# One level of Strassen in the gate and up projections of a decoder layer, with the down projection by tokens and its sum in DRAM

## The chip, the cores and the metric

The kernel runs on one core of one Trainium2 chip. The metric is the device time of one execution in microseconds (us). TensorE (PE) multiplies; a matmul holds a 128x128 stationary operand (loaded by a weight load, PEld) and streams a moving operand of up to 512 columns past it into one of eight PSUM banks. VectorE (DVE), ScalarE (ACT) and GpSimd (POOL) work on SBUF and PSUM; DMAs are issued from the queues of SyncE (SP), ACT and POOL.

## The reference

One layer of a decoder with 512 tokens, model width 2048, feed-forward width 5632, in fp32:

```python
x = x + concat(diff_attention(...), retention(...)) @ w_o       # from one combined projection w_in of rmsnorm(x)
x = x + cross_attention(rmsnorm(x), rmsnorm(mem)) @ w_xo        # 256 memory tokens, 4 heads
hf = rmsnorm(x, norm_ffn_g)
x = x + (silu(hf @ w_gate) * (hf @ w_up)) @ w_down
return rmsnorm(x, norm_f_g)
```

The change is in the feed-forward part, the third and fourth lines; its three weight matrices hold 3 x 2048 x 5632 numbers.

## The kernel before

**Precision.** Each fp32 operand is written as a sum of two `float32r` halves, `hi` (a rounded copy, made by ACT) and `lo` (the rest, made by DVE); `split` does it. A product is three matmuls, hi·hi, hi·lo and lo·hi (`mm3`, lines 129 to 131).

**Weights as a stream.** All weights are cut on the host into chunks of 128 x 1024 (512 KB), in the order in which they are used. `plan` is a list of chunks written out by the code at the end; `run_plan` goes through it. At chunk i it issues loads up to chunk i+5 (`raw`, four buffers, SP queue), splits up to chunk i+2 (`hi`, `lo`, three buffers each), then the matmuls of chunk i (`use`), then the evacuation of its banks if the chunk is the last of its group (`evac`), then one step of every side generator. Each engine runs its instructions in the order in which they are recorded here; semaphores do the rest.

**Stages.** Memory projections (matmuls with 256 moving columns), then eight heads with their projections ("mix"), cross attention, its output projection (`plan_xo`, 16 chunks), and the feed-forward part in eleven blocks b of 512 features. `plan_gate(b)` and `plan_up(b)` are 8 chunks each, `plan_down(b)` is 8 chunks in 4 groups. The order is gate(0), up(0), then gate(b), down(b-1), up(b) for b = 1 to 10.

**Feed-forward before.** Activations are feature-major: `xT[k]` holds 128 features by 512 tokens. In `feature_major` the stationary operand is a weight block and the moving operand is `ah[k]`/`al[k]` (the halves of `xT[k]` times the gain, 512 columns). A gate or up block takes 16 x 4 x 3 = 192 matmuls of 512 columns into four banks. The four gate banks are multiplied by `r_bc` (the norm's 1/rms, spread over partitions; DVE line 726), put through Silu (ACT 728) and multiplied by `r_bc` again (DVE 729); the up banks are multiplied by that (DVE 738) and split into `live["a"]`. `plan_down` is feature-major as well and adds each bank to the residual `xT[k]` (DVE 746). The last down block (b = 10) is left to `finish`: its weights are split by `last_weights` into `ah`/`al`, the residual is turned to token-major by 64 transposes (`turn_residual`), and 192 matmuls, token by token, give the rows that are normed and stored.

Of the kernel before, what the change touches and what calls it, by code (L numbers as in the profile page):

```python
# [35 lines left out]
LOADS_AHEAD = 6  # L36
# [4 lines left out]
LINE = 32  # L41
# [22 lines left out]
def hybrid_block_kernel(ctx, tc, specs, x_t, mem_t, gains, norm_f_g, weights, alibi, decay, out):  # L64
# [6 lines left out]
    res = ctx.enter_context(tc.tile_pool(name="res", bufs=1))  # L71
    wp = ctx.enter_context(tc.tile_pool(name="wp", bufs=1))
    dram = ctx.enter_context(tc.tile_pool(name="dram", bufs=1, space=DRAM))
    ps_acc = ctx.enter_context(tc.tile_pool(name="ps_acc", bufs=4, space=PSUM))
    ps_aux = ctx.enter_context(tc.tile_pool(name="ps_aux", bufs=4, space=PSUM))

    def acc(name="acc"):
        return ps_acc.tile([P, 512], F32, tag="acc", name=name)

    def aux(name="aux"):  # L80
        return ps_aux.tile([P, 512], F32, tag="aux", name=name)

    phase = ExitStack()
    mp = phase.enter_context(tc.tile_pool(name="mp", bufs=1))
# [6 lines left out]
    gc = const.tile([P, 96], F32, name="gc")  # L91
    nc.scalar.dma_start(out=gc[:, :NG], in_=gains)
    lam2 = const.tile([P, LINE], F32, name="lam2")[:, :2]
    elam = const.tile([P, LINE], F32, name="elam")[:, :2]
    lam = const.tile([P, LINE], F32, name="lam")[:, :1]
    gsub = const.tile([P, LINE], F32, name="gsub")[:, :2]

# [16 lines left out]
    def tmp():  # L114
        return wp.tile([P, T], F32, tag="tmp", name="tmp", bufs=2)
# [17 lines left out]
    def rsqrt(dst, ss, n, pool):  # L133

        w = dst.shape[-1]
        v = pool.tile([P, LINE], F32, tag="rs_v", name="rs_v")[:, :w]
        nh = pool.tile([P, LINE], F32, tag="rs_h", name="rs_h")[:, :w]
        y = pool.tile([P, LINE], I32, tag="rs_y", name="rs_y")[:, :w]
        t = pool.tile([P, LINE], F32, tag="rs_t", name="rs_t")[:, :w]
# [14 lines left out]
    def across(dst, cols):  # L154
# [7 lines left out]
        b_ps = aux("b_ps")  # L162
# [5 lines left out]
    def token_sums(dst, sq):  # L168

        s_ps = aux("s_ps")  # L170
# [6 lines left out]
    plan = []  # L177
    raws, halves, side = {}, {}, []
    count = {"load": 0, "split": 0}

# [3 lines left out]
    def load(i):  # L184
        raw = wp.tile([P, 1024], F32, tag="raw", name="raw", bufs=4)
        raws[i] = raw
        for a, b in pieces_of(i):
            nc.sync.dma_start(out=raw[:, a:b], in_=plan[i]["src"][:, a:b])

    def halve(i):  # L190
        raw = raws.pop(i)
        hi = wp.tile([P, 1024], F32R, tag="hi", name="hi", bufs=3)
        lo = wp.tile([P, 1024], F32R, tag="lo", name="lo", bufs=3)
        for a, b in pieces_of(i):
            split(hi[:, a:b], lo[:, a:b], raw[:, a:b])
        halves[i] = (hi, lo)
# [10 lines left out]
    def load_more(upto):  # L207
        while count["load"] < min(upto, len(plan)):
# [3 lines left out]
    def split_more(upto):  # L212
        while count["split"] < min(upto, len(plan)):
            halve(count["split"])
            count["split"] += 1

    def run_plan():
        for i, c in enumerate(plan):
            for f in c["early"]:
                f()  # L220
            load_more(i + LOADS_AHEAD)
            split_more(i + SPLITS_AHEAD)
            for f in c["before"]:
                f()
            c["use"](*halves.pop(i))
# [9 lines left out]
    def add(src, use, evac, hook):  # L235
        plan.append({"src": src, "use": use, "evac": evac, "hook": hook, "early": [], "before": [], "side": "after"})
# [34 lines left out]
    def token_major(w, width, nk_total, lhs_of, ntok, finish, hook=None, bank=acc):  # L271
# [3 lines left out]
        for k0 in range(0, nk_total, nk):  # L275
            last = k0 + nk >= nk_total

            def use(hi, lo, k0=k0, last=last):
# [8 lines left out]
                (lambda: [finish(t, banks[t]) for t in range(ntok)]) if last else None, hook if last else None)  # L287


    xT = [res.tile([P, T], F32, name=f"xT{k}") for k in range(KT)]  # L290
    ah = [res.tile([P, T], F32R, name=f"ah{k}") for k in range(KT)]
    al = [res.tile([P, T], F32R, name=f"al{k}") for k in range(KT)]
    ssq = const.tile([P, T], F32, name="ssq")
    rx = const.tile([P, LINE], F32, name="rx")[:, :NT]
    rxs = const.tile([P, LINE], F32, name="rxs")[:, :NT]
    g_d = dram.tile([HEADS // 2, KT // 2, P, 1024], F32, name="g_d")
    h_d = dram.tile([D // 512, HEADS, P, 1024], F32, name="h_d")

# [7 lines left out]
    mh = [mp.tile([P, MEM], F32R, name=f"mh{k}") for k in range(KT)]  # L306
    ml = [mp.tile([P, MEM], F32R, name=f"ml{k}") for k in range(KT)]
    rm = mp.tile([P, LINE], F32, name="rm")[:, :MT]
    rm_bc = mp.tile([P, MEM], F32, name="rm_bc")
# [8 lines left out]
    def start():  # L318
        for j in range(4):
            load_mem(j)  # L320
            load_more(j + 1)
# [9 lines left out]
    def mem_stats():  # L331
# [9 lines left out]
        sm2 = mp.tile([P, LINE], F32, name="sm2")[:, :MT]  # L341
        nc.vector.tensor_copy(sm2, s_ps[:, :MT])
        rsqrt(rm, sm2, D, mp)
# [6 lines left out]
    def plan_memory(h):  # L350
# [3 lines left out]
        def fin_x(name):  # L354
            def fin(o, ps):
                if o == 0:
                    xs[name] = (mp.tile([P, 4, MEM], F32R, tag=name + "h", name=name + "h", bufs=1),
                                mp.tile([P, 4, MEM], F32R, tag=name + "l", name=name + "l", bufs=1))
# [5 lines left out]
        for c in range(4):  # L364
            def fin_h(t, ps, c=c):
                if t == 0:
                    xs["h"] = mp.tile([P, 2, 512], F32, tag="mst", name="hst", bufs=3)
# [7 lines left out]
        for c in range(4):  # L375
            def fin_g(o, ps, c=c):
                if o == 0:
                    xs["g"] = mp.tile([P, 4, MEM], F32, tag="mst", name="gst", bufs=3)
# [15 lines left out]
    def prepare_x():  # L394
# [9 lines left out]
        st4 = wp.tile([P, LINE], F32, tag="st4", name="st4", bufs=1)[:, :NT]  # L404
        token_sums(st4, ssq)
        yield
        rsqrt(rx, st4, D, wp)
# [13 lines left out]
    pool = {}  # L421

    def half_pair(tag, shape, bufs=1):
        return (pool[0].tile(shape, F32R, tag=tag + "h", name=tag + "h", bufs=bufs),
                pool[0].tile(shape, F32R, tag=tag + "l", name=tag + "l", bufs=bufs))

# [3 lines left out]
    def plan_values(h):  # L430
# [5 lines left out]
        def fin_vg(t, ps):  # L436
            fin_v(t, ps)
            if t == 0:
                live["g", h] = pool[0].tile([P, NT, 256], F32, tag="gate", name="gate", bufs=1)
# [19 lines left out]

    def head_norm(om, ss):  # L460
        rs = pool[0].tile([P, LINE], F32, tag="rs", name="rs", bufs=1)[:, :NT]
        rsqrt(rs, ss, 256, pool[0])
        return rs
# [14 lines left out]
    def diff_head(h):  # L478
        qk = live["qk", h]
        tab = pool[0].tile([P, 640], F32, tag="tab", name="tab", bufs=1)  # L480
        nc.sync.dma_start(out=tab[:, :T], in_=alibi[h])
        om = pool[0].tile([P, NT, 256], F32, tag="om", name="om", bufs=1)
        ss = pool[0].tile([P, LINE], F32, tag="ss", name="ss", bufs=1)[:, :NT]
# [12 lines left out]
        def exps(i):  # L496
            n = (i + 1) * P
            e = pool[0].tile([P, 2, (P, 2 * P, T, T)[i]], F32, tag=("e3", "e1", "gate", "e3")[i], name="e", bufs=1)
            st = pool[0].tile([P, LINE], F32, tag="st", name="st", bufs=4)
# [45 lines left out]
        steps = ((0, scores), (3, turn), (5, values), (1, exps), (2, combine), (4, halve_weights), (6, collect))  # L545
# [12 lines left out]
    def ret_head(h):  # L558
        qk = live["qk", h]
        tab = pool[0].tile([P, 640], F32, tag="tab", name="tab", bufs=1)  # L560
        nc.sync.dma_start(out=tab, in_=decay[h - 4])
        om = pool[0].tile([P, NT, 256], F32, tag="om", name="om", bufs=1)
        ss = pool[0].tile([P, LINE], F32, tag="ss", name="ss", bufs=1)[:, :NT]
# [12 lines left out]
        for p in range(2):  # L576
            nj = 2 * p + 2
            i0 = p * 256
            st = pool[0].tile([P, nj, 256], F32, tag=("e1", "e3")[p], name="rst", bufs=1)
# [47 lines left out]
    prep = {"done": KT, "ready": 0, "gen": None}  # L627

    def prepare(at):
# [11 lines left out]
        st4 = wp.tile([P, LINE], F32, tag="st4", name="st4", bufs=1)[:, :NT]  # L641
        token_sums(st4, ssq)
        yield
        rsqrt(rx, st4, D, wp)
        nc.vector.tensor_scalar(out=rxs, in0=rx, scalar1=float(SX), scalar2=None, op0=ALU.mult)

    def start_prepare(at):
        prep["gen"] = prepare(at)
# [3 lines left out]
    def prepared_rhs(k):  # L652
        while prep["done"] <= k:
            next(prep["gen"])
        return ah[k], al[k]

# [3 lines left out]
    def plan_scores(p):  # L660
# [5 lines left out]
        def fin(t, ps):  # L666
            if t == 0:
                sc = pool[0].tile([P, 4, NT, 2], F32, tag="xst", name="xst", bufs=2)
                live["p", p] = (pool[0].tile([P, NT, 2, MEM], F32, tag="xe", name="xe", bufs=2), sc)
# [47 lines left out]
    turns = [0]  # L717

    def alternate():
        turns[0] += 1  # L720
        return (acc, aux)[turns[0] % 2 == 0]

    def plan_gate(b):
        def fin(o, ps):
            t = tmp()
            nc.vector.tensor_tensor(out=t, in0=ps, in1=live["r_bc"], op=ALU.mult)
            s = pool[0].tile([P, T], F32, tag=f"gs{o}", name="gs", bufs=1)
            nc.scalar.activation(s, t, AF.Silu)
            nc.vector.tensor_tensor(out=s, in0=s, in1=live["r_bc"], op=ALU.mult)
            live["s", o] = s  # L730
        feature_major(cols("w_gate", (b * 512, 512)), 512, KT, prepared_rhs, T, fin, bank=alternate())

    def plan_up(b):
        def fin(o, ps):
            if o == 0:
                live["a"] = half_pair("a", [P, 4, T])
            s = live["s", o]
# [185 lines left out]
```

## Time and profile before

| | |
|---|---|
| median of 3 runs | 2801.92 us (2801.42 to 2802.19) |
| the profiled execution | 2801.72 us, of which the span of the trace is 2799.9 us |
| TensorE | 2782.8 us busy (99%), 13910 matmuls |
| VectorE / ScalarE | 1290.0 us (46%) / 859.2 us (31%) |
| feed-forward part | from about 1337 us to the end |
| one block of it (gate, down, up) | 131.85 us |

How to read it: a matmul's own duration in the trace (391 ns for 512 columns) overlaps with the next one's, so what counts on TensorE is the distance from one start to the next. "Idle before" of an engine names what it waited for. Rows of a timeline begin with the start in us and the duration.

### The profile page before, as it was taken

What the parts mean: (1) busy time and instruction counts of PE and PEld (TensorE: products, weight loads), DVE (VectorE), ACT (ScalarE), POOL (GpSimd) and SP (SyncE); (2) the same over time, 40 slices, a digit from 0 to 9 for tenths busy, and PEclk for the clock granted to TensorE, in tenths of its full rate; (3) what the DMA queues carried; (4) which work ended last, traced back from release to release, by engine and by line L of the source; (5) the groups of instructions that cost most, each with busy time, mean ns of one, the idle gap of its engine ahead of it and who ended that gap; (6) DMA issues with size and microseconds to landing.
All of it is one profiled execution on the core that took longest, in us unless ns stands there. A gap on an engine that the chain in (4) does not pass through costs nothing.

```text
span 2799.9 us, 33522 instructions
## 1 busy us (share of the span) xinstructions
PE 2782.8 (99%) x13910; PEld 2358.7 (84%) x13910; DVE 1290.0 (46%) x1855; ACT 859.2 (31%) x1182; POOL 3.0 (0%) x10
## 2 busy tenths in 40 slices
PE   9999999999999999999999999999999999999998
PEld 8999988888888888888888888888888888888886
DVE  6676444544543444745433434343434243434356
ACT  5555433332322222434221212222222222222223
POOL 0000000000000000000000000000000000000000
PEclk9999999999999999999999999999999999999999
DMA  7877652222222222222223222222222222222241
GB/s 242 288 241 227 216 188 84 87 87 94 88 91 89 94 91 90 96 90 95 94 91 102 94 98 98 91 98 98 98 94 94 98 98 95 94 98 98 92 134 68
DMA packets 99192, 322.29 MB, mean 115 GB/s; under 512 B 10592, under 2 KB 20832, under 8 KB 99040
## 3 DMA queue, kind: packets, MB, share of 16 engines
q1 hardware_dynamic: 96272, 310.68, 33.4%
q10 hardware_dynamic: 2448, 8.43, 0.7%
q8 instruction: 109, 1.79, 0.3%
q0 software_dynamic: 320, 1.05, 0.1%
q14 instruction: 43, 0.35, 0.0%
HBM read 299.14 MB, written 20.97 MB: 114 GB/s over the span
## 4 chain that ended last, share of the span: by engine, by line
PE 98%; DVE 1%; ACT 0%; issue 0%; DMA 0%; ACTq 0%; DVEq 0%
PE fm L129 26%; PE fm L131 26%; PE fm L130 26%; PE tm L129 5%; PE tm L130 5%; PE tm L131 5%; PE y L130 1%; PE y L129 1%; PE y L131 1%; PE mx_ps L472 0%; PE y_ps L778 0%; DVE xT L620 0%; PE at_ps L523 0%; PE s_ps L130 0%; PE s_ps L129 0%; PE s_ps L131 0%
## 5 line engine op out<-in xcount | busy, mean ns | idle before, releaser
L121 DVE TENSOR_TENSOR lo<-raw,hi 128x1024 fp32r<-128x1024 f32 (+1 forms) x545 | 666.1, 1223 | 1211.9 <-ACT hi L120 1198.1
L120 ACT CAST hi<-raw 128x1024 fp32r<-128x1024 f32 (+1 forms) x545 | 572.1, 1050 | 1589.9 <-PE fm L130 1293.5
L129 PE MATMUL fm<-ah,hi 128*128 128x512 f32 x2432 | 951.6, 391 | 0.0
L131 PE MATMUL fm<-ah,lo 128*128 128x512 f32 x2432 | 950.3, 391 | 0.0
L130 PE MATMUL fm<-al,hi 128*128 128x512 f32 x2432 | 950.2, 391 | 0.0
L131 PEld LDWEIGHTS fm<-ah,lo 128*128 128x128 f32 x2432 | 456.5, 188 | 99.4
L129 PEld LDWEIGHTS fm<-ah,hi 128*128 128x128 f32 x2432 | 456.6, 188 | 98.2
L130 PEld LDWEIGHTS fm<-al,hi 128*128 128x128 f32 x2432 | 456.6, 188 | 98.1
L129 PE MATMUL tm<-hi,ah 128*128 128x512 f32 (+1 forms) x640 | 222.6, 348 | 0.6 <-DVE qkl L121 0.3
L130 PE MATMUL tm<-lo,ah 128*128 128x512 f32 (+1 forms) x640 | 221.9, 347 | 0.0
L131 PE MATMUL tm<-hi,al 128*128 128x512 f32 (+1 forms) x640 | 221.9, 347 | 0.0
L129 PE MATMUL fm<-mh,hi 128*128 128x256 f32 x512 | 146.5, 286 | 6.2 <-ACT hi L120 6.2
L131 PE MATMUL fm<-mh,lo 128*128 128x256 f32 x512 | 145.6, 284 | 0.0
L130 PE MATMUL fm<-ml,hi 128*128 128x256 f32 x512 | 145.5, 284 | 0.0
L746 DVE TENSOR_TENSOR xT<-xT,fm 128x512 f32<-128x512 f32 x160 | 109.8, 686 | 61.5 <-PE fm L131 56.9
L129 PEld LDWEIGHTS tm<-hi,ah 128*128 128x128 f32 x640 | 121.2, 189 | 16.0 <-issue 0.7
L131 PEld LDWEIGHTS tm<-hi,al 128*128 128x128 f32 x640 | 121.2, 189 | 15.1
L130 PEld LDWEIGHTS tm<-lo,ah 128*128 128x128 f32 x640 | 121.2, 189 | 14.6
L129 PEld LDWEIGHTS fm<-mh,hi 128*128 128x128 f32 x512 | 97.9, 191 | 6.4 <-ACT hi L120 6.2
L620 DVE TENSOR_TENSOR xT<-xT,fm 128x512 f32<-128x512 f32 x128 | 85.2, 683 | 32.4 <-PE fm L131 30.7
L131 PEld LDWEIGHTS fm<-mh,lo 128*128 128x128 f32 x512 | 97.7, 191 | 0.2 <-DVE lo L121 0.2
L130 PEld LDWEIGHTS fm<-ml,hi 128*128 128x128 f32 x512 | 97.8, 191 | 0.0
(202 smaller groups left out, 2426.4 us busy)
## 6 DMA issues: line engine op xcount, KB each, us to landing
raw<-in_weights_dram SPq DMA_DIRECT2D x519, 512.0 KB, 3.3
h_d<-hst ACTq DMA_DIRECT2D x16, 512.0 KB, 5.4
g_d<-gst SPq DMA_DIRECT2D x32, 256.0 KB, 3.6
raw<-g_d SPq DMA_DIRECT2D x16, 512.0 KB, 3.2
raw<-h_d SPq DMA_DIRECT2D x16, 512.0 KB, 3.2
xT<-in_x_t_dram SPq DMA_DIRECT2D x16, 256.0 KB, 5.0
out_dram<-xT SPq DMA_DIRECT2D x16, 256.0 KB, 2.6
xT<-in_mem_t_dram SPq DMA_DIRECT2D x8, 256.0 KB, 6.9
```

The costliest lines, as they stand in the source:

```text
L120: nc.scalar.copy(hi, src)
L121: nc.vector.tensor_tensor(out=lo, in0=src, in1=hi.bitcast(F32), op=ALU.subtract)
L129: nc.tensor.matmul(out_ap, lh, rh, start=first, stop=False)
L130: nc.tensor.matmul(out_ap, lh, rl, start=False, stop=False)
L131: nc.tensor.matmul(out_ap, ll, rh, start=False, stop=last)
L620: nc.vector.tensor_tensor(out=xT[k], in0=xT[k], in1=ps, op=ALU.add)
L746: nc.vector.tensor_tensor(out=xT[k], in0=xT[k], in1=ps, op=ALU.add)
```

## The change

**Gate and up.** Let the activations be cut into halves of the contraction (two k tiles of a pair j) and halves of the tokens, and the weights into halves of the contraction and of the 512 output columns. The four block products of each gate or up block become seven products of half size (`PRODUCTS`). Each uses one of seven sums of weight quarters and one of seven sums of activation quarters. `combine_weights` makes the weight sums of each chunk (DVE 266, 268, 269) and splits all seven (ACT 267, 270; DVE 271, 272), 1792 columns in place of 1024. `prepare_pairs` makes the activation sums once for all blocks. `seven_products` then issues 42 matmuls of 256 columns per chunk (7 products x 2 output tiles x 3 halves; the seven results lie in seven PSUM banks), where there were 24 of 512 columns. At the end of a block the four quarters of the result are put together from the seven banks (line 899 and 902 on DVE, one copy on ACT), for gate in `fin` with the norm and Silu in the side generator `activate`, for up in `fin` and `rest_of`.

**Down.** `token_major`: the stationary operand is the activation `a`, the moving one the weights (512 columns, as many matmuls as before). ACT takes each bank to SBUF times `rx` (line 974), into one of the two buffers of `tmp`, and a DMA on the POOL queue adds it to `y_d` in DRAM (line 975, `accum_op`), 16 per block. `xT` is turned to token-major and written to `y_d` once, by `turn_x` during `plan_xo` and gate(0). `plan_down(NB - 2)` now comes after up(10), with the last block's weights split between its last chunks (`plan_last`); `finish` loads the sums from `y_d`.

**Areas.** The tiles of the pools are replaced by hand-laid areas: `ops` (matmul operands) and `rest`. The halves of a chunk have two places of 14 KB in the feed-forward part until chunk 3 of up(0), three from there on (`place_for`); `raw` has three buffers after the memory stage (four before). PSUM banks are taken round in turn. The areas of the 256-column moving operands begin 32 bytes off; in the built program the address of a moving operand less that of the next weights is, modulo 256 bytes, 32 for all of `seven_products` and 0 for all 512-column matmuls. In the program before it was 0 for gate and up, and 128 for down, `pt`, `mx` and the last products `y`.

TensorE at the end of up(0) and the start of gate(1), before (`ah`, `al`: moving activations, `hi`, `lo`: weights):

```order
7789 L129 MATMUL fm<-ah_121,hi 128x512
7790 L130 MATMUL fm<-al_137,hi 128x512
7791 L131 MATMUL fm<-ah_121,lo 128x512
7792 L129 MATMUL fm<-ah_106,hi 128x512 [waits Activation_49]
7793 L130 MATMUL fm<-al_122,hi 128x512
7794 L131 MATMUL fm<-ah_106,lo 128x512 [waits DVE_49]
7795 L129 MATMUL fm<-ah_106,hi 128x512
```

The same place of the changed kernel (`bank_70` to `bank_77` are the eight banks, `third` is the third place of halves):

```order
7670 L888 MATMUL bank_76<-ops 128x256 x6
7671 L888 MATMUL bank_77<-ops,third 128x256 [waits Activation_49]
7672 L888 MATMUL bank_77<-ops,third 128x256
7673 L888 MATMUL bank_77<-ops,third 128x256 [waits DVE_49]
7674 L888 MATMUL bank_77<-ops,third 128x256 x3
7675 L888 MATMUL bank_70<-ops,third 128x256 [waits Activation_49]
7676 L888 MATMUL bank_70<-ops,third 128x256 x5
7677 L888 MATMUL bank_71<-ops,third 128x256 [waits DVE_49]
```

The matmuls are half as wide, six to a bank, and gate(1) goes into the one free bank and then into those that up(0) has just filled, each as it is evacuated.

VectorE at the same place, before: the evacuation of up (738, with the split of `a`) and the splits of the next chunks.

```order
1084 L738 TENSOR_TENSOR gs<-fm,gs 128x512 [waits PE_49]
1085 L121 TENSOR_TENSOR al<-gs,ah 128x512 [waits Activation_49]
1086 L121 TENSOR_TENSOR lo<-raw,hi 128x1024 [waits DMAHW4_49,Activation_49]
1087 L121 TENSOR_TENSOR lo<-raw,hi 128x1024 [waits DMAHW5_49,PE_49,Activation_49]
1088 L121 TENSOR_TENSOR lo<-raw,hi 128x1024 [waits DMAHW6_49,PE_49,Activation_49]
```

VectorE between up(1) and gate(2), changed: the end of `fin` (902, 899), the five instructions of one chunk's sums and halves, the first of `rest_of`, the next chunk.

```order
1350 L902 SCALAR_TENSOR_TENSOR rest<-bank_73,rest 128x512 [waits PE_49]
1351 L899 TENSOR_TENSOR u_10492<-u_10492,bank_74 128x512 [waits DVE_49,PE_49]
1352 L266 TENSOR_TENSOR rest<-rest 128x512 [waits DMAHW4_49]
1353 L268 TENSOR_TENSOR rest<-rest 128x256 [waits DVE_49]
1354 L269 TENSOR_TENSOR rest<-rest 128x256 [waits DVE_49]
1355 L271 TENSOR_TENSOR ops<-rest,ops 128x768 [waits Activation_49]
1356 L272 TENSOR_TENSOR ops<-rest,ops 128x1024 [waits Activation_49]
1357 L182 TENSOR_TENSOR a_l<-rest,a_h 128x2x256 [waits Activation_49]
1358 L899 TENSOR_TENSOR rest<-rest 128x2x256
1359 L182 TENSOR_TENSOR a_l<-rest,a_h 128x2x256 [waits Activation_49]
1360 L266 TENSOR_TENSOR rest<-rest 128x512 [waits DMAHW5_49]
```

Five instructions stand where one stood, and the putting together of up stands between the chunks of gate.

ScalarE in a down block, changed: four evacuations to `tmp` (974) of a group, then the casts of the next chunks. Before, ACT had only casts here.

```order
812 L974 ACTIVATE rest<-bank_72,small 128x512 [waits DMASW2_49,PE_49,Activation_49]
813 L974 ACTIVATE rest<-bank_73,small 128x512 [waits DMASW3_49,PE_49,Activation_49]
814 L974 ACTIVATE rest<-bank_74,small 128x512 [waits DMASW4_49,PE_49,Activation_49]
815 L974 ACTIVATE rest<-bank_75,small 128x512 [waits DMASW5_49,PE_49,Activation_49]
816 L181 CAST ops<-rest 128x1024 [waits DMAHW0_49]
817 L181 CAST third<-rest 128x1024 [waits DMAHW1_49,DVE_49,PE_49]
818 L974 ACTIVATE rest<-bank_76,small 128x512 [waits DMASW6_49,PE_49,Activation_49]
```

Each evacuation now waits for the POOL DMA (DMASW) of the evacuation two before it, and the casts of later chunks stand behind it.

The diff, cut to its core:

```diff
+PRODUCTS = ((0, 0), (2, 2), (5, 5), (3, 4), (4, 3), (6, 1), (1, 6))
 def tmp():
-        return wp.tile([P, T], F32, tag="tmp", name="tmp", bufs=2)
+        return part(rest, F_TMP + take("tmp", 2) * 2 * KB, [P, T])
...
+    def combine_weights(raw, hi, lo):
+        q = raw.rearrange("p (a b) -> p a b", b=256)
+        w = phased("tw", [P, 4, 256])
+        nc.vector.tensor_tensor(out=w[:, 0:2], in0=q[:, 1:3], in1=q[:, 0:1].to_broadcast([P, 2, 256]), op=ALU.add)
+        nc.scalar.copy(hi[:, 0:3], q[:, 1:4])
+        nc.vector.tensor_tensor(out=w[:, 2], in0=w[:, 0], in1=q[:, 2], op=ALU.add)
+        nc.vector.tensor_tensor(out=w[:, 3], in0=w[:, 2], in1=q[:, 3], op=ALU.add)
+        nc.scalar.copy(hi[:, 3:7], w)
+        nc.vector.tensor_tensor(out=lo[:, 0:3], in0=q[:, 1:4], in1=hi[:, 0:3].bitcast(F32), op=ALU.subtract)
+        nc.vector.tensor_tensor(out=lo[:, 3:7], in0=w, in1=hi[:, 3:7].bitcast(F32), op=ALU.subtract)
...
+    def prepare_pairs(at):
+        prep.update(done=0, ready=0, free=5)
+        for j in range(KT // 2):
+            while prep["ready"] <= 2 * j + 1 or prep["free"] <= j:
+                yield
...
+    def seven_products(w, finish, hook=None):
...
+                for n, (a, b) in enumerate(PRODUCTS):
...
+                    for o in range(2):
+                        c = slice(o * P, (o + 1) * P)
+                        to = banks[n][:, o * 256:(o + 1) * 256]
+                        for m, (x, y) in enumerate(((hi, sh), (hi, sl), (lo, sh))):
+                            nc.tensor.matmul(to, x[:, b, c], y[:, a], start=j == 0 and o == 0 and m == 0,
+                                             stop=j == nj - 1 and m == 2, skip_group_check=True)
...
     def plan_down(b):
         for c0 in range(0, D, 512):
-            def fin(o, ps, c0=c0):
-                k = c0 // P + o
-                nc.vector.tensor_tensor(out=xT[k], in0=xT[k], in1=ps, op=ALU.add)
-                prep["ready"] = k + 1
-            feature_major(cols("w_down", (c0, 512), row0=b * 512), 512, 4,
-                          lambda k: sub(live["a"], slice(None), k), T, fin, bank=alternate())
+            def fin(t, ps, c0=c0):
+                st = tmp()
+                nc.scalar.activation(st, ps, AF.Copy, scale=rx[:, t:t + 1])
+                nc.gpsimd.dma_start(out=y_d[t * P:(t + 1) * P, c0:c0 + 512], in_=st, accum_op=ALU.add)
+            token_major(cols("w_down", (c0, 512), row0=b * 512), 512, 4, lhs, NT, fin, bank=any_bank, ffn=True)
...
     for b in range(1, NB):
         plan_gate(b)
-        plan_down(b - 1)
+        plan_down(b - 1) if b < NB - 1 else None
         plan_up(b)
+    plan_down(NB - 2)
+    plan_last()
```

More of the change, by code (lines that the diff above doesn't have):

```diff
@@ L174, in token_sums @@
         nc.vector.tensor_copy(dst, s_ps[:, :n])
-    plan = []
+    plan, items = [], []
     raws, halves, side = {}, {}, []
     count = {"load": 0, "split": 0}
+    raw_free = [part(rest, F_RAW + n * 4 * KB, [P, 1024]) for n in range(3)]
+    raw_free.append(part(rest, F_PHASE + 12 * KB, [P, 1024]))
+    raw_mem = raw_free[3]
+    places = {"whole": [(n * 8 * KB, 8 * KB, None) for n in (0, 1, 2)], "seven": [(n * 14 * KB, 14 * KB, None) for n in (0, 1)]}
+    held = {}
     def pieces_of(i):
@@ new lines, in place_for @@
+    def place_for(c):
+        kind = "seven" if c["ffn"] else "whole"
+        for n, (at, size, own) in enumerate(places[kind]):
+            if all(o is not own or at + size <= a or a + z <= at for a, z, o in held.values()):
+                places[kind].append(places[kind].pop(n))
+                return at, size, own
+        return None
+    def combine_weights(raw, hi, lo):
[8 more added lines that the diff above has]
+        nc.vector.tensor_tensor(out=lo[:, 3:7], in0=w, in1=hi[:, 3:7].bitcast(F32), op=ALU.subtract)
@@ new lines, in halve @@
+    def halve(i):
+        c = items[i]
+        if c["to"] is not None:
+            for (hi, lo), b in zip(c["to"], (0, 512)):
+                split(hi, lo, raws[i][:, b:b + 512])
+        else:
+            place = place_for(c)
+            if place is None:
+                return False
+            held[i] = place
+            at, size, own = place
+            n = 1792 if c["kind"] == "seven" else 1024
+            hi = part(own or ops, at, [P, n])
+            lo = part(own or ops, at + size // 2, [P, n])
+            if c["kind"] == "seven":
+                hi, lo = shaped(hi, [P, 7, 256]), shaped(lo, [P, 7, 256])
+                combine_weights(raws[i], hi, lo)
+            else:
+                for a, b in pieces_of(i):
+                    split(hi[:, a:b], lo[:, a:b], raws[i][:, a:b])
+            halves[i] = (hi, lo)
+        raw = raws.pop(i)
+        if raw is not raw_mem or count["load"] + len(raw_free) < count["mem"]:
+            raw_free.append(raw)
+        return True
@@ L205, in drain, with load_more @@
             step_side()
[L207 to L208 removed]
+    def load_more():
+        while raw_free and count["load"] < len(items):
             load(count["load"])
@@ L303, in act_lhs @@
         return ah[k][:, t * P:(t + 1) * P], al[k][:, t * P:(t + 1) * P]
[L306 to L309, printed above, removed]
+    mh = [part(ops, R_TAGS["mh"][0] + k * KB, [P, MEM]) for k in range(KT)]
+    ml = [part(ops, R_TAGS["ml"][0] + k * KB, [P, MEM]) for k in range(KT)]
+    rm_bc = phased("rm_bc", [P, MEM])
     def load_mem(j):
@@ L655, in prepared_rhs, with prepared_pair @@
         return ah[k], al[k]
+    def prepared_pair(j):
+        while prep["done"] <= j:
+            next(prep["gen"])
+        return pairs[j]
     marks = []
@@ new lines, in plan_last, with finish @@
+    def plan_last():
+        tail = items[-5:]
+        del items[-5:]
+        for j in range(KT // 2):
+            if j < 5:
+                plan[-5 + j]["item"] = len(items)
+                items.append(tail[j])
+            src = chunk("w_down", (NB - 1) * 512 + j % 2 * 256, 2, [(j // 2 * 512, 512)])
+            items.append({"src": src, "kind": "whole", "ffn": True,
+                          "to": [(wh[2 * j + n], wl[2 * j + n]) for n in range(2)]})
+    def finish():
+        top.close()
+        ypool = top.enter_context(tc.tile_pool(name="ypool", bufs=1))
+        ys = [ypool.tile([P, D], F32, name=f"y{t}") for t in range(NT)]
+        for t in range(NT):
+            nc.sync.dma_start(out=ys[t], in_=y_d[t * P:(t + 1) * P, :])
+        gain = phased("gs", [P, 4, T])
```

433 lines of the change are left out of this document (273 added, 160 removed).

## The prediction

> **What bounds the kernel now.** First the page: the busy times, the row of TensorE in 40 slices and the chain that ended last.
>
> ```profile
> span 2799.9 us, 33522 instructions
> PE 2782.8 (99%) x13910; PEld 2358.7 (84%) x13910; DVE 1290.0 (46%) x1855; ACT 859.2 (31%) x1182; POOL 3.0 (0%) x10
> PE   9999999999999999999999999999999999999998
> PE 98%; DVE 1%; ACT 0%; issue 0%; DMA 0%; ACTq 0%; DVEq 0%
> ```
>
> TensorE is busy in every slice and is 98% of the chain. What matters first is how many matmuls are issued and how far apart. Next, the windows: up(0), gate(1) and a whole block (down, up, gate), cut where the first evacuation of a stage starts on DVE.
>
> ```profile
> 1416.88 0.68 DVE L738 TENSOR_TENSOR gs<-fm,gs 128x512 f32<-128x512 f32 x1
> 1460.39 0.68 DVE L726 TENSOR_TENSOR tmp<-fm,r_bc 128x512 f32<-128x512 f32 x1
> ```
> ```profile
> core 0: us, PE busy (x) PEld busy (x) DVE busy (x) ACT busy (x) POOL busy (x), PEclk, DMA share, GB/s
> 1373.36:1416.88 43.52, 43.52 (x193) 36.05 (x193) 14.97 (x18) 10.98 (x13) 0.00 (x0) 1.00 0.29 97
> 1416.88:1460.39 43.51, 43.51 (x193) 36.04 (x193) 14.96 (x17) 10.82 (x12) 0.00 (x0) 1.00 0.29 97
> 1460.39:1592.24 131.85, 131.85 (x578) 108.11 (x577) 50.40 (x57) 30.08 (x32) 0.00 (x0) 1.00 0.29 96
> ```
>
> An up or gate stage is 192 matmuls in 43.51 us, 0.2266 us each, at a granted clock of 1.00. The block leaves 131.85 - 87.03 = 44.82 us for down, 0.2335 each: as many matmuls as wide, and slower. The last products `y` show the same second rate.
>
> ```profile
> 2745.65 0.40 PE L129 MATMUL y<-ah,ah 128*128 128x512 f32 x1
> 2790.04 0.40 PE L131 MATMUL y<-ah,al 128*128 128x512 f32 x1
> ```
>
> These are the first and last of 192: 44.39 / 191 = 0.2324. The operands' addresses differ modulo 256 by 128 there and in down, by 0 in gate. So TensorE is the bound, and DVE (15 of 43.5 us in gate) and ACT (11) have room; DMA runs at 0.29 of its engines' time.
>
> **The change, part by part.** The sum is made against the profiled execution, 2801.7 us, which the median (2801.9) matches.
>
> *Gate and up, 22 stages.* 192 matmuls of 512 columns become 336 of 256. The trace has 256-wide ones in the memory stage:
>
> ```profile
> 13.28 0.28 PE L129 MATMUL fm<-mh,hi 128*128 128x256 f32 x1
> 31.79 0.28 PE L129 MATMUL fm<-mh,hi 128*128 128x256 f32 x1
> 268.07 0.35 PE L129 MATMUL fm<-xkh,hi 128*128 128x256 f32 x1
> 274.03 0.36 PE L129 MATMUL fm<-xkh,hi 128*128 128x256 f32 x1
> ```
>
> The first two are 156 matmuls apart, and the accumulator changes every third: 18.51 / 156 = 0.1187. The other two are 48 apart with a new group's start between: 5.96 / 48 = 0.1242. I take 0.1187, since the new stream also changes banks (every sixth) and starts a group once a stage. A stage is then 336 x 0.1187 = 39.88 us, and 22 x (43.51 - 39.88) = **-80 us**. At 0.1242 it would be 41.73 and only -39. If the 32-byte offset, which no row of before has, made the price of a column that of the 512-wide matmul (0.1133), -120. No reason excludes either.
>
> [...]
>
> *512-wide matmuls at offset 0.* Down keeps its 192 per block, at 0.2266 in place of 0.2335: 10 x 1.33 = -13 us. The 192 of `y`, 768 of `mx` and 384 of `pt` had offset 128 as well: 1344 x (0.2324 - 0.2266) = -8 us. **-21 us**; if the offset is not the cause, 0.
>
> *VectorE between up and gate.* Durations:
>
> ```profile
> L121 DVE TENSOR_TENSOR lo<-raw,hi 128x1024 fp32r<-128x1024 f32 x543 | 664.8, 1225 | 1211.9 <-ACT hi L120 1198.1 <-PE mx_ps L472 12.6 <-PE y_ps L778 0.3
> L120 ACT CAST hi<-raw 128x1024 fp32r<-128x1024 f32 x543 | 570.9, 1052 | 1589.9 <-PE fm L130 1293.5 <-PE tm L131 159.6 <-issue 103.9
> L738 DVE TENSOR_TENSOR gs<-fm,gs 128x512 f32<-128x512 f32 x44 | 30.1, 683 | 0.0
> L379 DVE TENSOR_TENSOR gst<-fm,rm_bc 128x256 f32<-128x256 f32 x64 | 22.5, 414 | 0.0
> L392 DVE TENSOR_TENSOR ssq<-ssq,tmp 128x512 f32<-128x512 f32 x52 | 35.6, 684 | 2.5 <-ACT tmp L391 2.2
> L391 ACT ACTIVATE tmp<-xT 128x512 f32<-128x512 f32 x52 | 32.6, 626 | 5.5 <-DVE ssq L392 5.0 <-ACT hst L368 0.4
> L368 ACT ACTIVATE hst<-tm,rm 128x512 f32<-128x512 f32 x32 | 22.0, 688 | 16.5 <-PE tm L131 16.5
> ```
>
> Chunk's sums and halves: 0.68 + 2 x 0.41 + 0.95 (768 columns, between 0.68 and 1.23) + 1.23 = 3.7 us of DVE, against a chunk of TensorE of 42 x 0.1187 = 4.99. ACT needs 0.84 + 1.05 = 1.9 (768 columns between 0.63 and 1.05). In a gate and up pair DVE has 16 x 3.7 for chunks and 22 x 0.68 (15 and 7) for the two `fin` and `rest_of`, 74.2 of 79.8 us, so the cover is thin. The tight place is the order quoted for VectorE. Taken from TensorE's end of up: the split of gate chunk 1 has been able to run since chunk 6 of up left its place, 4.99 us earlier, and ends at -1.3; `fin`'s eight instructions (0.68 each) end at 4.2; three chunk splits (11.1), `rest_of`'s seven (4.8) and two waits for ACT's halves of `a` (0.63 each, 512 columns) bring the `lo` of gate chunk 4 to 21.4. TensorE wants it 4 x 4.99 + 0.24 = 20.2 us after the end (its third matmul uses it). 1.2 late, ten times: **+12 us** (0 if the sums run ahead of the place, 40 if every instruction after another on DVE costs 0.1 more: 28 of them).
>
> *Start of the feed-forward part.* `prepare_pairs` costs DVE a chunk's 3.7 and two squares (1.37) for each of eight pairs; five are made ahead, three fall into gate(0). There only two places for halves exist, so every two chunks DVE has 12.5 us of work in 10.0 of TensorE: 3 x 2.5 = 7.5. The evacuation of up(0) with two places, by the same count, 3.5; `turn_x` on a fuller ACT in `plan_xo`, 2. **+13 us** (5 to 20).
>
> *The accumulating DMAs.* Before has no DMA that adds. Nearest rows, of 256 KB:
>
> ```profile
> raw<-in_weights_dram SPq DMA_DIRECT2D x519, 512.0 KB, 3.3
> g_d<-gst SPq DMA_DIRECT2D x32, 256.0 KB, 3.6
> out_dram<-xT SPq DMA_DIRECT2D x16, 256.0 KB, 2.6
> xT<-in_norm_f_g_dram POOLq DMA_DIRECT2D x4, 256.0 KB, 7.4
> ```
>
> A store takes 2.6 us on idle queues and 3.6 among loads; the one POOL row, a burst of four, takes 7.4. Let L be the time from issue to landing. ACT's evacuation n waits for the DMA of n - 2, so two take 0.69 + L. The first bank of down is full 36.7 us before its end (a group is 48 x 0.2266 = 10.9, and its first bank is done 4.1 before the group's end), its evacuation ends at -36.0, and the fifteenth's at -36.0 + 7 (0.69 + L). Its bank is wanted by the seventh product of the up stage behind it, 6 x 0.71 = 4.3 us after the end. TensorE thus waits 7 L - 35.5 per block, from L = 5.1 on; ACT's casts stand behind these evacuations and are late with them. I take 3.6, the loaded store, and 0.7 for data that is read as well as written (512 KB against 256: 3.3 - 2.6): L = 4.3, **0 us**, hidden beneath the next group of down. At 2.6 it is 0 too; at 7.4, 16.3 x 10 = +163.
>
> *The end.* `finish` loads 4 MB of sums, under 44 us of last products. The rows behind, from the last matmul to the end of the span, are as before:
>
> ```profile
> 2790.48 0.69 DVE L800 TENSOR_TENSOR y<-y,y 128x512 f32<-128x512 f32 x1 [1.39 <-PE y L131]
> ```
>  The residual's 64 transposes go from the end to `plan_xo`: they were TensorE's before and stay so, 0. **+1 us**, for the first load.
>
> Sum: -80 - 21 + 12 + 13 + 0 + 1 = -75, so 2801.7 - 75 = **2727 us**.
>
> **The rivals.**
>
> *The ring decides: slower.* If L is over (73 / 10 + 35.5) / 7 = 6.1 us, waiting for two `tmp` buffers eats the gain: 6.4 gives +93 - 75, 2820; 7.4 gives 2890. For it: the one POOL row. Against: those four were issued together, and both rows of stores lie under 4.
>
> *The ring binds in part.* L between 5.1 and 6.1, 2727 to 2797. One way to it: each DMA is held until the running DVE instruction ends, at most 1.2 us: L = 5.5, 3 us a block, 2757. The Trainium skill, "SBUF — State Buffer", section "Who interferes with whom", says that DVE in a two-port mode locks GpSimd out, which writes the descriptors of such DMAs, but that `tensor_tensor` has no such mode. By that there is no holding, and no run yet shows either.
>
> *256-wide matmuls cost 0.1242.* +41: 2768. For it only rows at group starts.
>
> *DVE becomes the bound of gate and up.* The five instructions of a chunk form a chain in which most wait for the one before; 0.12 us of that for each of 80 is 9.6 us a pair, 4.0 past the 5.6 of room, and 11 x 4.0 = +44: 2771. Against: the durations of such rows in before hold the writing of the result, and no row shows a wait of DVE for itself.
>
> **How the numbers follow.** A difference under 0.2% (5.6 us) is about what a measurement of this kernel can't tell from none. Chances: as forecast 0.55 (2700 to 2755), ring in part 0.16, ring decides 0.15, matmul price 0.05, DVE 0.09. All but the deciding ring are faster, less 0.03 for a ring just at the break-even: faster 0.82, same 0.03, slower 0.15. The range goes from 2685 (matmuls at 0.1133 without the late `lo`: 2727 - 40, and a little) to 2810, where the ring's worse half is left out.
>
> **What would show it.** A gate stage of 39.9 us and 336 matmuls; down at 43.5; in the waits of TensorE some 1 us ten times for DVE at line 272, and none for ACT at line 974; POOL's DMAs landing in 4 to 5 us; DVE near 75% busy over the feed-forward part. Wrong it is if line 974 waits for POOL's DMAs and TensorE for line 974, or if 256-wide starts lie 0.124 apart.

## The result, and the profile after

The changed kernel takes 2818.55 us (median of 4 runs, 2818.07 to 2819.09) against 2801.79 us of the kernel before on the same chip: 1.006 times as long, 95% interval 1.0042 to 1.0077. The forecast was 2727 us and "faster". The profiled execution took 2818.68 us.

The page of the changed kernel first, the rows that answer to those of before:

```profile
span 2816.3 us, 41803 instructions
PE 2707.0 (96%) x17078; PEld 2449.3 (87%) x17078; DVE 1679.0 (60%) x2494; ACT 1122.0 (40%) x1550; POOL 150.4 (5%) x186
PE   9999999999999999999998999998989989999997
PE 46%; issue 41%; DVE 5%; POOL 5%; ACT 2%; DMA 1%; POOLq 0%; ACTq 0%; DVEq 0%
```

TensorE is busy 76 us less than before, and yet the span is 16 us longer: the rest of the span, the idle time of TensorE, has grown from 17 to 109 us. POOL, which was not in the chain of work that ended last, is now 5% of it. What TensorE and ScalarE waited for (the waits view: us in total, times, longest):

```profile
PE bank L888 <- ACT rest L974: 56.4, 21, 5.4
PE bank L888 <- DVE ops L271: 5.8, 10, 0.9
```
```profile
ACT rest L974 <- DMA y_d<-rest: 268.4, 114, 7.1
```

That is the chain that the forecast called the deciding ring: TensorE waits for the evacuation of down, and the evacuation for the adding DMA of the one two before. The DMA rows of the page, in KB each and median us from issue to landing, and the group of their issues:

```profile
y_d<-rest POOLq DMA_DIRECT2D x176, 256.0 KB, 5.4
```
```profile
L975 POOL DMA_DIRECT2D y_d<-rest x160 | 138.7, 881 | 1271.3 <-ACT rest L974 1151.0 <-DVE ops L182 116.9 <-issue 2.2
```

They land in 5.4 us, not the 4.3 of the sum (the row counts in 16 plain writes of the start, which land in 2.7; the 160 adding ones alone have a median of 5.6). One block from the timeline, ScalarE's first and some of its last evacuations, POOL's issue behind the one of 1640.90, and TensorE after them (start, duration; the matmuls of the seven products stand as groups, "x24"):

```profile
1607.85 0.69 ACT L974 ACTIVATE rest<-bank,small 128x512 f32<-128x512 f32 x1 [0.27 <-PE bank L192]
...
1640.90 0.69 ACT L974 ACTIVATE rest<-bank,small 128x512 f32<-128x512 f32 x1 [4.21 <-DMA y_d<-rest]
...
1648.44 1.26 ACT L974 ACTIVATE rest<-bank,small 128x512 f32<-128x512 f32 x2
1654.85 0.69 ACT L974 ACTIVATE rest<-bank,small 128x512 f32<-128x512 f32 x1 [5.14 <-DMA y_d<-rest]
```
```profile
1641.88 0.86 POOL L975 DMA_DIRECT2D y_d<-rest  x1 [4.03 <-ACT rest L974]
```
```profile
1644.37 3.12 PE L888 MATMUL bank<-ops 128*128 128x256 f32 x24
1649.17 1.68 PE L888 MATMUL bank<-ops 128*128 128x256 f32 x12 [1.69 <-ACT rest L974]
1655.59 4.62 PE L888 MATMUL bank<-ops 128*128 128x256 f32 x24 [4.74 <-ACT rest L974]
1659.82 3.22 PE L888 MATMUL bank<-ops 128*128 128x256 f32 x26
```

From the first evacuation to the fifteenth (1654.85) are 47.0 us, seven steps of 6.71. Down ended at 1644.37; up got through its first four products and stood still for its fifth bank and again for its seventh. The matmuls behind the second halt are slow as well. (The last two rows are of windows that meet at 1660 us, and two matmuls are in both.) From 1655.59 to 1659.82 are 22 steps, 0.192 us each, where the next 25 are 0.118. The windows say why; the first two are 12 matmuls behind the halt of 1.69 us and the first 3.4 us behind that of 4.74, then come up and gate, down, up and gate:

```profile
core 0: us, PE busy (x) PEld busy (x) DVE busy (x) ACT busy (x) POOL busy (x), PEclk, DMA share, GB/s
1649.17:1650.85 1.68, 1.68 (x12) 1.47 (x12) 1.61 (x3) 0.53 (x1) 1.43 (x2) 1.00 0.84 266
1655.73:1659.14 3.41, 3.41 (x17) 3.41 (x18) 1.59 (x2) 3.03 (x4) 1.73 (x2) 0.50 0.72 80
1644.37:1732.28 87.91, 81.49 (x674) 80.92 (x673) 70.39 (x98) 35.84 (x44) 3.49 (x4) 0.98 0.45 125
1732.28:1775.83 43.55, 43.55 (x194) 36.04 (x193) 13.11 (x16) 16.55 (x22) 10.24 (x12) 1.00 0.68 136
1775.83:1864.15 88.32, 82.38 (x673) 81.41 (x672) 70.72 (x98) 36.39 (x44) 3.60 (x5) 0.94 0.47 123
```

An up and the gate behind it take 88 us, of which 6 are waits, and the mean granted clock is 0.98 and 0.94 there: behind the halt of 4.74 us it is 0.50 for 3.4 us, while behind the halt of 1.69 it stays at 1.00. Down itself, between them, takes 43.55.

### The profile page after: what moved, and what is told of

Read it like the earlier page. It is cut to its first block, busy times and chain, and to the rows that moved or that the text cites. A ratio compares the mean times of both kernels' runs of the same rounds, so it can differ in the third digit from the quotient of the medians.

```text
span 2816.3 us, 41803 instructions
## 1 busy us (share of the span) xinstructions
PE 2707.0 (96%) x17078; PEld 2449.3 (87%) x17078; DVE 1679.0 (60%) x2494; ACT 1122.0 (40%) x1550; POOL 150.4 (5%) x186
## 3 DMA queue, kind: packets, MB, share of 16 engines
q0 software_dynamic: 24640, 47.20, 11.4%
## 4 chain that ended last, share of the span: by engine, by line
PE 46%; issue 41%; DVE 5%; POOL 5%; ACT 2%; DMA 1%; POOLq 0%; ACTq 0%; DVEq 0%
PE bank L190 15%; PE bank L192 15%; PE bank L191 15%; POOL y_d L975 5%; PE bank L888 1%; ACT ops L270 1%; DMA y_d<-rest 1%; DVE ops L272 1%; DVE rest L266 0%; DVE y L1018 0%; DVE rest L899 0%; DVE ops L182 0%; DMA rest<-in_norm_f_g_dram 0%; DVE rest L268 0%; DVE rest L269 0%
## 5 line engine op out<-in xcount | busy, mean ns | idle before, releaser
L190 PE MATMUL bank<-ops 128*128 128x512 f32 (+1 forms) x2504 | 858.4, 343 | 12.6 <-ACT ops L181 7.2
L191 PE MATMUL bank<-ops 128*128 128x512 f32 (+1 forms) x2504 | 851.3, 340 | 0.8 <-DVE ops L182 0.8
L192 PE MATMUL bank<-ops 128*128 128x512 f32 (+1 forms) x2504 | 851.7, 340 | 0.0
L182 DVE TENSOR_TENSOR ops<-rest,ops 128x1024 fp32r<-128x1024 f32 (+1 forms) x380 | 449.8, 1188 | 630.8 <-ACT ops L181 617.3
L888 PE MATMUL bank<-ops 128*128 128x256 f32 x5208 | 650.6, 285 | 66.1 <-ACT rest L974 56.4
L888 PEld LDWEIGHTS bank<-ops 128*128 128x128 f32 x5208 | 635.6, 193 | 76.6 <-ACT rest L974 60.8
L181 ACT CAST ops<-rest 128x1024 fp32r<-128x1024 f32 (+1 forms) x380 | 386.0, 1022 | 686.1 <-PE bank L191 354.1
L190 PEld LDWEIGHTS bank<-ops 128*128 128x128 f32 x2504 | 473.4, 189 | 69.1 <-ACT ops L181 8.1
L192 PEld LDWEIGHTS bank<-ops 128*128 128x128 f32 x2504 | 472.7, 189 | 53.8 <-DVE ops L182 0.2
L191 PEld LDWEIGHTS bank<-ops 128*128 128x128 f32 x2504 | 473.2, 189 | 52.8 <-DVE ops L182 1.4
L888 PE MATMUL bank<-ops,third 128*128 128x256 f32 x2184 | 265.5, 280 | 2.7 <-ACT rest L941 1.6
L888 PEld LDWEIGHTS bank<-ops,third 128*128 128x128 f32 x2184 | 260.4, 189 | 3.1 <-ACT rest L941 1.8
L271 DVE TENSOR_TENSOR ops<-rest,ops 128x768 fp32r<-128x768 f32 x124 | 118.2, 953 | 102.6 <-ACT ops L267 88.4
L272 DVE TENSOR_TENSOR ops<-rest,ops 128x1024 fp32r<-128x1024 f32 x124 | 152.0, 1226 | 31.0 <-ACT ops L270 29.2
L190 PE MATMUL bank<-ops,a_h 128*128 128x512 f32 x408 | 160.2, 393 | 4.0 <-ACT ops L181 4.0
L191 PE MATMUL bank<-ops,a_h 128*128 128x512 f32 x408 | 160.1, 393 | 0.5 <-DVE ops L182 0.5
L192 PE MATMUL bank<-ops,a_l 128*128 128x512 f32 x408 | 159.7, 391 | 0.0
```

The costliest lines, as they stand in the source:

```text
L181: nc.scalar.copy(hi, src)
L182: nc.vector.tensor_tensor(out=lo, in0=src, in1=hi.bitcast(F32), op=ALU.subtract)
L190: nc.tensor.matmul(out_ap, lh, rh, start=first, stop=False)
L191: nc.tensor.matmul(out_ap, lh, rl, start=False, stop=False)
L192: nc.tensor.matmul(out_ap, ll, rh, start=False, stop=last)
L271: nc.vector.tensor_tensor(out=lo[:, 0:3], in0=q[:, 1:4], in1=hi[:, 0:3].bitcast(F32), op=ALU.subtract)
```

## The experiments

The theory after the comparison: the two `tmp` buffers, through the time of the adding DMA. Its rivals: the DMAs' traffic slows everything, whatever the buffers; or VectorE, whose work grew by 390 us, is the limit and the ring only comes with it.

**Five and three buffers.** `u` and `u3` hold sums of up and are idle during down, so they can take evacuations:

```diff
+    sums = [lambda n=n: part(rest, F_TMP + n * 2 * KB, [P, T]) for n in range(2)]
+    sums += [lambda: shaped(live["u"].rearrange("p a b -> p (a b)"), [P, T])]
+    sums += [lambda n=n: part(rest, F_PHASE + (12 + n * 2) * KB, [P, T]) for n in range(2)]
...
-                st = tmp()
+                st = sums[take("sum", 5)]()
```

(and `3` in the other run). In both, the last down block follows up(10) directly and takes these places while sums of up(10) are still wanted, so block 10 is not the reference's share there; the instructions are the same in number and kind.

> The down evacuations take turns over five buffers instead of two (the three more are the areas of up's sums, idle during down). Theory (ring): ACT's evacuation waits for the DMA two before it, TensorE for the bank; with five the wait of TensorE for line 974 (56 us) goes to under 5, a stretch of up and gate falls from 88.3 to 79 to 81 us, the time to about 2725. Rival (traffic): the adding DMAs themselves slow DMA, ACT or TensorE, whatever the buffers; then the stretch stays above 86 and the time above 2795. Rival (VectorE): the sums and halves of the weights are the limit, the ring only comes with them; then the stretch stays near 85, the time near 2785.

> Three buffers. Ring: an evacuation comes 6.7 us after the one two before it now; with three the fifteenth of a block is free four such steps after the third, before its own bank is full, so nearly all is gained: 2725 to 2740. Traffic and VectorE: as with five, above 2780.

Five: 2716.31 us (2714.85 to 2716.9), 0.9697 of before (0.9683 to 0.9711), 9 us below the time expected. No wait of TensorE for the evacuation of down is left; what its seven products wait for most is this:

```profile
PE bank L888 <- DVE ops L271: 3.9, 4, 1.4
```

Three: 2748.85 us, 0.9812 (0.9796 to 0.9828), faster than before by some 1.9% and 9 us above the range expected. The expectation took the step of two buffers, and it did not hold: with three each DMA takes longer, 6.0 us and more where it was 5.4. The DMA rows of the run with three, and what ScalarE (the same evacuation is line 979 here) and TensorE waited for:

```profile
y_d<-rest POOLq DMA_DIRECT2D x123, 256.0 KB, 6.0
y_d<-u POOLq DMA_DIRECT2D x53, 256.0 KB, 6.4
```
```profile
ACT rest L979 <- DMA y_d<-rest: 128.6, 33, 7.1
ACT u L979 <- DMA y_d<-u: 62.7, 16, 5.8
```
```profile
PE bank L888 <- DVE ops L271: 14.8, 13, 1.4
```

With three, ScalarE still waits 191 us for landings, in place of 268. Its casts stand behind these waits, VectorE's halves behind the casts, and TensorE waits for VectorE where it waited for the bank: for 1.26 to 1.42 us in each of the eight gates, every time at the third matmul of the gate's fifth chunk. An up and gate then takes 80 to 82 us, and the end of the kernel, from the last down's start, 117 us in place of 105 with five. The traffic theory falls: the same DMAs, with the same bytes, cost TensorE nothing in up, gate and down when there are five buffers. So does the theory that VectorE is the limit of the changed kernel: with the same sums an up and gate takes 78.6 us there, not 85.

**What makes the DMA long.** Two buffers, but a plain write, from POOL's queue and from SP's; the sum over the blocks is left out in both.

```diff
-  nc.gpsimd.dma_start(out=y_d[t * P:(t + 1) * P, c0:c0 + 512], in_=st, accum_op=ALU.add)
+  nc.gpsimd.dma_start(out=y_d[t * P:(t + 1) * P, c0:c0 + 512], in_=st)      # or nc.sync
```

> Two buffers as in the changed kernel, but the DMA on POOL's queue writes in place of adding (the sum over blocks is left out). If the adding makes the DMA long, it lands in 3.6 us or less, the stretch of up and gate falls to 81 and the time to 2730; if POOL's path does, it lands in 5 and more and the time stays above 2790.

> The same plain write, from SP's queue behind the weight loads (the sum over blocks is left out). By the row of such stores in the kernel before (3.6 us among loads) the ring no longer binds: 2730. If SP's issues stand in order behind loads that wait for a buffer, the write is held and the time is nearer 2800.

From POOL 2719.2 us, 11 below the time expected, from SP 2727.2 (one run each). The rows of the first, then of the second:

```profile
y_d<-rest POOLq DMA_DIRECT2D x176, 256.0 KB, 3.3
```
```profile
L975 POOL DMA_DIRECT2D y_d<-rest x160 | 86.3, 540 | 1225.3 <-ACT rest L974 1220.5 <-issue 3.8
```
```profile
y_d<-rest SPq DMA_DIRECT2D x160, 256.0 KB, 3.8
```

So it is the adding and not the queue that makes the DMA long: 3.3 us against 5.4 to landing, and 0.54 against 0.88 us for POOL to issue one. POOL's path is even shorter than SP's (3.8 us), so the second half of the last expectation (issues held behind loads) shows at most in the 8 us between the two. The packets agree: POOL's queue moved the same 47.20 MB in 24640 packets with adding and in 14400 without, in 11.4% against 4.5% of the engines' time (changed kernel, then the plain write).

```profile
q0 software_dynamic: 24640, 47.20, 11.4%
```
```profile
q0 software_dynamic: 14400, 47.20, 4.5%
```

The Trainium skill, "DMA: Bandwidth & Descriptors", section "Anatomy of one DMA — SWDGE (gpsimd) path", gives 2.0 us and the bytes by 436 GB/s; by that 256 KB are estimated at 2.6 us. The median of these plain writes from POOL is 3.3, and the formula does not tell an adding DMA from a plain one, which the runs do.

**The version that can be used.** Five buffers for blocks 0 to 8; for the last block two `tmp` and the 4 KB of the weight sums, which are no longer needed.

```diff
+                n = take("sum", 5 if b < NB - 2 else 4)
+                st = sums[n]() if b < NB - 2 or n < 2 else part(rest, F_PHASE + (n - 2) * 2 * KB, [P, T])
```

> Five buffers for the evacuations of the down blocks 0 to 8, four (other) ones for the last, whose places up's sums still need. Nothing else is changed against the run with five. Ring: 2714 to 2720, no wait of TensorE for the evacuation of down.

2715.38 us (2714.13 to 2718.47), 0.9692 of before (0.9675 to 0.9709): faster than both kernels, with nothing of the computation left out, and as expected. Its windows, an up and gate and the down behind:

```profile
1755.10:1833.78 78.68, 78.68 (x674) 78.64 (x672) 63.99 (x88) 31.90 (x38) 1.60 (x2) 1.00 0.41 120
1833.78:1877.32 43.54, 43.54 (x194) 36.04 (x193) 20.46 (x25) 21.17 (x27) 12.27 (x15) 1.00 0.78 172
```

No idle time, clock 1.00, 78.68 / 672 = 0.1171 us for a matmul. Eight blocks side by side, from the start of up(1) to that of up(9), first in the changed kernel, then in this one:

```profile
1511.17 0.50 PE L888 MATMUL bank<-ops 128*128 128x256 f32 x2
2569.37 0.89 PE L888 MATMUL bank<-ops 128*128 128x256 f32 x6
```
```profile
1510.65 1.22 PE L888 MATMUL bank<-ops 128*128 128x256 f32 x9
2487.97 1.22 PE L888 MATMUL bank<-ops 128*128 128x256 f32 x9
```

1058.2 us against 977.3, and 8 x 131.85 = 1054.8 before the change. The ring took 10.1 us a block, the slower clock behind its halts counted in: all that the seven products bring (9.7) and a little more.

**Where the operands lie.** Built on the last one:

```diff
-R_PAIRS = R_ACT + 32
+R_PAIRS = R_ACT
...
-                live["a"] = [part(ops, R_ACT + n * 8 * KB, [P, 4, T]) for n in range(2)]
+                live["a"] = [part(ops, R_ACT + 128 + n * 8 * KB, [P, 4, T]) for n in range(2)]
```

> As the run with five and four buffers, but the activation sums of the seven products lie 32 bytes lower (moving address less next weights: 0 modulo 256 in place of 32), and the stationary halves of the last products 128 bytes higher (128 in place of 0). If the offset sets a matmul's price: 256 columns go from 0.1168 to 0.119 to 0.120 us, the time up by 16 to 24 us, and the last products from 0.2266 to 0.2324, +1 us. If it does not: both spacings and the time stay within 3 us.

2733.65 us (2733.01 to 2734.74), 0.9759 of before (0.9744 to 0.9775), 18 us above the version that it is built on. An up and gate takes 80.63 / 672 = 0.1200 us a matmul at offset 0. The last products, at 128, lie 23.01 / 99 = 0.2324 apart, where the changed kernel at 0 has 0.2267 (16.32 / 72, by the same kind of rows):

```profile
1759.73:1840.36 80.63, 80.63 (x674) 80.63 (x672) 64.11 (x88) 31.89 (x38) 1.60 (x2) 1.00 0.40 118
```
```profile
2691.80 0.40 PE L192 MATMUL bank<-ops 128*128 128x512 f32 x1
2714.81 0.40 PE L192 MATMUL bank<-ops 128*128 128x512 f32 x1
```

Both moves did what the offset's theory said, the first of a moving operand, the second of a stationary one. The 18 us are of both together: 2.0 in each up and gate, and about 1 was expected of the last products. Other differences, and whether 256 bytes is the period, were not tried.

**How much room VectorE has.** The usable version with the first sum of each chunk made twice:

```diff
         nc.vector.tensor_tensor(out=w[:, 0:2], in0=q[:, 1:3], in1=q[:, 0:1].to_broadcast([P, 2, 256]), op=ALU.add)
+        nc.vector.tensor_tensor(out=w[:, 0:2], in0=q[:, 1:3], in1=q[:, 0:1].to_broadcast([P, 2, 256]), op=ALU.add)
```

> As the run with five and four buffers, with the first weight sum of each chunk made twice: 0.69 us more of VectorE per chunk, 11 us per up and gate. By the prediction's count (74.2 of 79.8 us were VectorE's) it becomes the bound: +5 to +7 us a pair, 2770 to 2790. By the busy time traced with five buffers (64 of 78.5 us) it still fits: within 5 us, unless the order at the evacuation of up makes a wait, then up to +3 us a pair, 2745.

2770.74 us (one run), the low end of the first expectation's range; the second falls. Eleven microseconds more of work cost 82.74 - 78.6 = 4.1 a pair, less than the 5 to 7 expected; the time is in the range because gate(0), up(0) and gate(1) take 14 us more as well. The window, and two rows of the waits:

```profile
1778.13:1860.87 82.74, 80.23 (x674) 80.02 (x673) 72.62 (x102) 32.49 (x38) 1.60 (x2) 0.98 0.38 113
```
```profile
ACT ops L271 <- DVE rest L270: 235.1, 103, 7.0
PE bank L889 <- DVE ops L272: 31.0, 14, 3.0
```

VectorE reads 72.62 of 82.74 us, and TensorE waits for it all the same: 2.5 us in each gate, again at the third matmul of the fifth chunk; the other 1.6 us of the 4.1 are the clock, 0.98 here. ScalarE's cast waits for VectorE's sums (235 us, where the version with five and four buffers has 122; the extra line moves numbers by one), VectorE's own subtraction waits for the cast, and three chunks of up are prepared under down. Busy time in the window understates it.

## Why the prediction was wrong, point by point

The measured time lies 9 us above the range and 92 above the forecast. By the prediction's own steps, in us, the measured ones as distances between starts in TensorE's timeline:

| | forecast | changed | five and four buffers |
|---|---|---|---|
| gate(0), up(0), gate(1) | 131.8 | 135.8 | 136.0 |
| up and gate, mean of eight | 81.0 | 88.4 | 78.6 |
| down, mean | 43.5 | 43.8 | 43.6 |
| up(9), gate(10), up(10) | 120.8 | 128.1 | 121.9 |
| from the last down's start to the end | 97.7 | 118.9 | 106.6 |

- *The step that failed* is the term of the accumulating DMAs: "L = 4.3, 0 us, hidden beneath the next group of down". The formula for the ring held, but its L was too small. By the block shown, a step is 0.69 + L = 6.71, so the formula's L is 6.02. Of that 5.46 are the DMA from issue to landing (the mean of the seven), 0.39 two hand-overs that the sum did not count (0.29 from ScalarE's end to POOL's issue, 0.10 from the landing to ScalarE), and the rest one evacuation that stood behind a cast. 7 x 6.02 - 35.5 = 6.6 us of waiting, where the timeline shows 1.69 + 4.74. The adding was priced by the bytes, 0.7; against the plain write from the same queue it costs 2.3 (5.6 against 3.3), of which 0.34 are POOL's issue.
- *What the formula left out* is the clock: the eight stretches of up and gate have 81.7 us of busy TensorE in the mean, in place of 78.6. In the block shown 17 matmuls behind the second halt, most of them at a clock of 0.50, take 1.6 us more than they would at 0.117. So the break-even lay lower than L = 6.1. By its L the case is the rival "the ring binds in part" (0.16), by its time "the ring decides" (0.15), at 6.4 of that scale. Neither of the rows that were weighed gave the right L: 3.6 for the stores, 7.4 for POOL's burst.
- *Gate and up*: right in kind, and better than forecast, 0.117 in place of 0.1187 (13 us). The 32-byte offset, which no row of before had, is the cheaper one, as the offsets run shows. 0.1242 was wrong.
- *512 columns at offset 0*: down at 43.55, forecast 43.5, and the last products by the offsets run: right. For `mx` and `pt` 6.7 us of gain were forecast too, but nothing is left of it where the feed-forward part begins: at 1331.7 us, and at 1331.2 before the change (not 1337, as the table of before has it). What took it up was not tried; most of the transposes of `turn_x` lie ahead of that point now.
- *VectorE between up and gate*: 12 us forecast, ten waits of 1.2. With five buffers there is none, the case of "0 if the sums run ahead of the place". With three buffers it is there, where the sum put it (gate chunk 4, counted from 0, third matmul) and of its size, 1.26 to 1.42 us, and with the doubled sum it is 2.5. The count of 74.2 us was right if the work under down is added (64.0 in the window of up and gate, and of down's 20.46 the 8.2 that neither its eight splits at 1.225 nor the norm's two products explain: 72); the thin cover is real, as the doubled sum shows. In the changed kernel no wait is seen at that place. For the 0.12 us of the rival on VectorE no row was given; with five and four buffers the idle time before the second and third sum of a chunk is 0.03.
- *Start*: 13 forecast; 135.8 against three stages of 39.3 (half of 78.6) are 18, in both versions nearly the same.
- *The end*: +1 was forecast; the part from the last down on takes 21 us more than its 97.7. The last down takes 51.5 us in place of 43.5: TensorE waits 4.0 us for a cast that stands behind two evacuations, and the clock is 0.93. Then "under 44 us of last products" overlooked that each of the four loads of `y_d` waits for the last adding DMA of its rows; the first is issued 0.07 us behind that landing. Changed kernel, the queue of SP and VectorE's first use:

```profile
2764.45 12.72 SPq L999 DMA_DIRECT2D y<-y_d  x4
```
```profile
2771.54 0.75 DVE L1018 SCALAR_TENSOR_TENSOR y<-bank,small,y 128x512 f32<-128x512 f32 x1 [11.95 <-DMA y<-y_d]
```

The last products began at 2749.0; the first load is issued 15.5 us later and has landed at 2771.4, when 88 of the 192 matmuls have begun. VectorE works off its part behind them, TensorE waits 2.6 us for a bank, and from the start of the last matmul to the end it is 16.9 us (2799.4 to 2816.3) in place of 9.9. With five and four buffers 9 of the 21 us remain. How that part divides between the landing of the last DMAs and the loads was not tried.

The other way to a longer L, a DMA held while VectorE runs, does not show in POOL's issue: in blocks 0 to 8 it takes 0.54 us for a plain write and 0.87 for an adding one, both when VectorE is busy for over nine tenths of it (39 and 25 of 144 issues) and when it is busy for less than one tenth (77 and 88). The Trainium skill, "SBUF — State Buffer", section "Who interferes with whom", says that VectorE shuts GpSimd out in its two-port modes, and that `tensor_tensor` has none. The issue times agree: nearly all of VectorE's instructions here are of that kind. Whether VectorE lengthens the landing of the adding DMAs was not tested by itself: by the same split they land in 5.8 against 5.3 us in the changed kernel, and in 5.8 against 6.1 with five and four buffers.

## What to carry to other kernels

A ring of buffers behind a DMA has a period: evacuation, hand-over, issue, landing, hand-over, divided by the number of buffers. Compare it with the time in which the banks fill, and price a DMA that adds as another operation than a store, or buy the doubt away with a third to fifth buffer when an area lies idle. A halt of TensorE can cost more than its length: here the 4.74 us brought 3.4 us at half the clock, the 1.69 us none. And where a profile shows two prices for one shape of matmul, look at the addresses.

## What the hardware showed that was not expected

- A DMA of 256 KB that adds to DRAM, the adding ones alone: a median of 5.6 us with two buffers, 6.4 with three, 6.1 with five, against 3.3 for a plain write from the same queue.
- The price of a matmul by the moving operand's address less that of the next weights (counted modulo 256 bytes; three differences were seen): 0.117 us at 32 and 0.120 at 0 for 256 columns in the same stream; 0.2267 at 0 and 0.2324 at 128 for 512.
- After a halt of 2.6 us in the last products eight matmuls of 512 columns take 3.42 us in place of 1.81; the granted clock is 0.50 from 2778.7 to 2782.1 us:

```profile
2778.93 0.79 PE L190 MATMUL bank<-ops 128*128 128x512 f32 x1 [2.61 <-DVE y L1018]
2779.52 0.63 PE L191 MATMUL bank<-ops 128*128 128x512 f32 x1
...
2782.08 0.43 PE L191 MATMUL bank<-ops 128*128 128x512 f32 x1
2782.35 0.40 PE L192 MATMUL bank<-ops 128*128 128x512 f32 x1
```
